# Rests of the tap matrices on one engine, and a gated channel tile split before it is put into token phases

## The chip, the core and the metric

One core of a Trainium2 chip runs the whole program. The metric is the device time of one execution in microseconds; the kernel before takes 1811.5 us (median of 3 runs, 1810.97 to 1811.91). TensorE does matrix products, VectorE, ScalarE and GpSimd elementwise work, SyncE issues the loads of the weights.

## The reference, cut to what matters

Two blocks of a model follow each other on 512 tokens of width 1024, all in fp32. The part that the change touches is the conformer convolution in the first block:

```python
def conformer_conv(h, w_pw1, b_pw1, w_dw, b_dw, ln_g, ln_b, w_pw2, b_pw2):
    u = h @ w_pw1 + b_pw1
    a, g = jnp.split(u, 2, axis=-1)
    u = a * jax.nn.sigmoid(g)
    u = depthwise_conv(u, w_dw) + b_dw        # 31 taps over the tokens, each channel by itself
    u = jax.nn.silu(layer_norm(u, ln_g, ln_b))
    return u @ w_pw2 + b_pw2
```

## The kernel before

Tensors lie with channels on the 128 partitions and the 512 tokens along the row, so 1024 channels are eight channel tiles. To get fp32 accuracy from the faster fp32r products, each factor is held as a head (rounded to fp32r by a ScalarE copy) and a rest (the value minus its head, a subtraction); a product is three matmuls, head by head, head by rest, rest by head (lines 358 to 360). `split` (line 392) makes such a pair of an activation: ScalarE writes the head (398), VectorE the rest (399).

Weights come in blocks of 512 columns, four 128-column pieces each. One load on SyncE (272) brings two blocks, 512 KB, into one of three `raw` buffers. For each block ScalarE copies the head into one of nine `W` buffers (285), and VectorE or GpSimd subtracts to give the rest (287); `on_pool` names the blocks whose rests GpSimd makes. A `raw` buffer is free when head and rest of both its blocks are made. The instructions of an engine are laid out ahead of time by a planner that works from the order of the program text, and run in that order.

The stage in question runs from about 649 to 772 us:

- TensorE multiplies by `pw1` (channel tiles 2 to 7, two gemms of 24 matmuls each, 512 columns). Behind each pair, `glu` multiplies both results by the row scales (1135, 1136), takes the sigmoid (451, called from 1137), and adds the bias and gates.
- Channel tiles 0 to 3 are convolved on VectorE: 31 instructions each (1078, 1083), handed out in small portions by `tick`. The first portions fall between the `pw1` gemms, the others between the tap matmuls.
- Channel tiles 4 to 7 are convolved on TensorE by `run_pe` after the last `pw1` gemm: tap matrices (`taps`, 128 pieces in 32 blocks, in 16 loads) multiply the gated tile. For that, even and odd tokens of 64 channels lie one above the other on the 128 partitions (two token phases, half as many columns: 256). Each tile takes 2 halves x 16 matrices x 3 = 96 matmuls of 256 columns; ScalarE then writes the sums back with the bias (1130, four instructions a tile).
- `conv_pe` prepares these tiles. Before the change VectorE gates straight into the phases (1111, four instructions on 64 partitions x 256), ScalarE takes the head of the whole (1113) and VectorE the rest (1114).
- The layer norm follows: TensorE adds up the columns of all eight tiles (1181) as soon as the last of them is written, ScalarE scales this to the mean (1192), and so on up to the `pw2` gemms.

Before the change GpSimd makes the rests of all `pw1` blocks from channel tile 2 on and of every second block of tap matrices; VectorE makes those of the other 16 blocks and of all later ones.

Of the kernel before, what the change touches and what calls it, by code (L numbers as in the profile page):

```python
# [11 lines left out]
F32 = mybir.dt.float32  # L12
F32R = mybir.dt.float32r
BF16 = mybir.dt.bfloat16
I32 = mybir.dt.int32
AF = mybir.ActivationFunctionType
OP = mybir.AluOpType
# [142 lines left out]
def pack(plan):  # L160

    blocks, cols = [[]], 0
    for piece in plan:
        if cols + piece[3] > 512:
            blocks.append([])
            cols = 0
        blocks[-1].append(piece)
        cols += piece[3]
    return [blocks[:1], blocks[1:2]] + [blocks[i:i + 2] for i in range(2, len(blocks), 2)]
# [75 lines left out]
class Weights:  # L245
# [4 lines left out]
    def __init__(self, prog, blob, raw_pool, w_pool):  # L250
        self.prog, self.nc, self.blob, self.raw_pool, self.w_pool = prog, prog.nc, blob, raw_pool, w_pool
        self.loads, self.blocks, self.loc, off = [], [], {}, 0
        for load in pack(make_plan()):
            start = 0
            for blk in load:
                c = 0
                for name, k, t, w in blk:
                    self.loc[name, k, t] = (len(self.blocks), c, w)
                    c += w
                self.blocks.append((len(self.loads), start, c))  # L260
                start += c
            self.loads.append((off, start))
            off += 128 * start
        self.raw, self.w, self.ndma, self.nsplit, self.cur = {}, {}, 0, 0, -1

        tiles = [self.loc["pw1", 7, 9][0] + 1, self.loc["taps", 0, 0][0], self.loc["pw2", 0, 0][0]]
        self.on_pool = set(range(tiles[0], tiles[1])) | set(range(tiles[1], tiles[2], 2))

    def dma(self):
        off, cols = self.loads[self.ndma]  # L270
# [34 lines left out]
class Program:  # L305
# [757 lines left out]
    def conformer(self, x, h, ps4, rs, first):  # L1063
        nc = self.nc
        V, A, G, mm, W = nc.vector, nc.scalar, nc.gpsimd, nc.tensor.matmul, self.W
        vv = self.pairs()
        late, mixed = [], []

        def conv_dve(c, up, dst, taps, bias):

            box = {}

            def tap(t):
                w, u = self.v("dw", 31 * c + t), up[:, t:t + T]
                if t == taps[0]:
                    acc = box["acc"] = self.PS()
                    if bias:
                        V.tensor_scalar(out=acc, in0=u, scalar1=w, scalar2=self.v("bdw", c), op0=OP.mult, op1=OP.add)
                    else:
                        V.tensor_scalar(out=acc, in0=u, scalar1=w, scalar2=None, op0=OP.mult)  # L1080
                else:
                    acc = box["acc"]
                    V.scalar_tensor_tensor(out=dst if dst is not None and t == taps[-1] else acc, in0=u, scalar=w,  # L1083
                                           in1=acc, op0=OP.mult, op1=OP.add)

            return [lambda t=t: tap(t) for t in taps], box

        def conv_pool(c, up, dst, taps):
            def tap(t):
                w, u = self.v("dw", 31 * c + t), up[:, t:t + T]  # L1090
                if t == taps[0]:
                    A.activation(out=dst, in_=u, func=AF.Identity, scale=w, bias=self.v("bdw", c))
                    return
                p = self.S()[:, :T]
                A.activation(out=p, in_=u, func=AF.Copy, scale=w)
                G.tensor_add(out=dst, in0=dst, in1=p)

            return [lambda t=t: tap(t) for t in taps]

        def conv_pe(c, a, g):  # L1100


            up = self.wide(F32)[:, :544].rearrange("p (h t) -> p h t", h=2)
            uh, ul = (self.wide(F32R)[:, :544].rearrange("p (h t) -> p h t", h=2) for _ in range(2))
            G.memset(up[:, :, 0:8], 0.0)
            G.memset(up[:, :, 263:272], 0.0)
            a, g = (x.rearrange("p (t f) -> p f t", f=2) for x in (a, g))
            for i in range(2):
                r = slice(64 * i, 64 * i + 64)
                for o, f, t in ((slice(0, 64), 1, 8), (slice(64, 128), 0, 7)):  # L1110
                    V.scalar_tensor_tensor(out=up[o, i, t:t + 256], in0=a[r, f], scalar=self.v("bp1", c)[r],
                                           in1=g[r, f], op0=OP.add, op1=OP.mult)
            A.activation(out=uh, in_=up, func=AF.Copy)
            V.tensor_sub(out=ul, in0=up, in1=uh.bitcast(F32))
            late.append((c, uh, ul))

        def run_pe():
            for i, (c, uh, ul) in enumerate(late):
                sums = self.PS().rearrange("p (h t) -> p h t", h=2)
                for g in range(2):  # L1120
                    for s in range(16):
                        self.mm3(sums[:, g], W("taps", s, 2 * i + g), (uh[:, g, s:s + 256], ul[:, g, s:s + 256]),
                                 s == 0, s == 15)
                        if s % 8 == 7:
                            self.tick(*TICK2)
                out = vv[c].rearrange("p (t f) -> p f t", f=2)
                for g in range(2):
                    for b in range(2):
                        r = slice(64 * b, 64 * b + 64)
                        A.activation(out=out[64 * g:64 * g + 64, b], in_=sums[r, g], func=AF.Identity,  # L1130
                                     bias=self.v("bd2", 2 * i + g)[r])

        def glu(c, za, zg):
            a, g = self.S()[:, :T], self.S()[:, :T]
            V.tensor_mul(out=g, in0=zg, in1=rs)  # L1135
            V.tensor_mul(out=a, in0=za, in1=rs)
            self.fn(SIGMOID, out=g, in_=g, func=AF.Sigmoid, bias=self.v("bp1", 8 + c))
            if CONV[c] == "E":
                return conv_pe(c, a, g)
            up = self.wide(F32)  # L1140
            G.memset(up[:, 0:15], 0.0)
            G.memset(up[:, 527:542], 0.0)
            V.scalar_tensor_tensor(out=up[:, 15:527], in0=a, scalar=self.v("bp1", c), in1=g,
                                   op0=OP.add, op1=OP.mult)
            if CONV[c] == "P":
                self.bg2.append(conv_pool(c, up, vv[c], range(31)))
            elif CONV[c] == "V":
                self.bg.append(conv_dve(c, up, vv[c], range(31), True)[0])
            else:
                self.bg2.append(conv_pool(c, up, vv[c], range(MIX)))  # L1150
                taps, part = conv_dve(c, up, None, range(MIX, 31), False)
                self.bg.append(taps)
                mixed.append((c, part))
# [3 lines left out]
        rs = rs()  # L1157
        self.tables(SIGMOID)
        glu(0, ps4[0], ps4[1])
        glu(1, ps4[2], ps4[3])  # L1160
        for c in range(2, 8):
            if c > 2:
                za = self.PS()
                self.gemm(za, "pw1", c, h)
                self.tick(*TICK)
            zg = self.PS()
            self.gemm(zg, "pw1", 8 + c, h)
            glu(c, za, zg)
            self.tick(*TICK)
        run_pe()  # L1170
        self.drain()
        for c, part in mixed:
# [570 lines left out]
```

## Time and profile before

| | |
|---|---|
| median of 3 runs | 1811.5 us |
| the profiled execution | 1812.31 us |
| its span, first to last instruction | 1810.6 us |
| TensorE busy | 1757.6 us, 97% |
| VectorE busy | 1113.1 us, 61% |
| ScalarE busy | 792.1 us, 44% |
| GpSimd busy | 250.6 us, 14% |

In the views PE is TensorE's matmul, PEld its weight load, DVE VectorE, ACT ScalarE, POOL GpSimd, SP SyncE (SPq its queue). `L287` is line 287. Busy shares are means over a program of many stages, so a stage is read with the views of its own stretch. Instructions of one engine overlap a little at their ends: what one costs in a row of the same kind is the distance from start to start, slightly less than its duration. The records of one execution give the durations; that execution took 0.8 us more than the median of the runs.

### The profile page before, as it was taken

Reading aid. Unit: us, or ns where it says so; the run is one execution under the profiler, and the core shown is the slowest. Engines: PE = TensorE matmul, PEld = TensorE weight load, DVE = VectorE, ACT = ScalarE, POOL = GpSimd, SP = SyncE. Lnnn points to the kernel's source line nnn. Section 1 sums busy time; section 2 is a strip of 40 time slices with the busy share of each in tenths; the row PEclk is TensorE's granted clock in tenths of the full one; section 3 lists DMA queues with packets and bytes.
Section 4 is the critical chain, followed back from the end, with each engine's and each line's share of the span. In section 5 each row is a group of like instructions: output and inputs, shape, how many; then the busy total and the mean of one; then the engine's idle time right before and its main releaser. Section 6 shows DMA issues by size and latency. Waiting matters only on the chain.

```text
span 1810.6 us, 23137 instructions
## 1 busy us (share of the span) xinstructions
PE 1757.6 (97%) x8828; PEld 1463.8 (81%) x8828; DVE 1113.1 (61%) x1798; ACT 792.1 (44%) x1445; POOL 250.6 (14%) x315
## 2 busy tenths in 40 slices
PE   9999999999999998999999999989999999999999
PEld 7778888888888976888888888888687888888887
DVE  7988685344444889967634444477997554344442
ACT  6546554333333532485533332346665433232330
POOL 3413330000000452303000000033223200000000
PEclk9999999999999999999999999999999999999999
DMA  6232223222222131421322222222222222222221
GB/s 202 64 99 65 94 71 105 93 96 99 97 93 94 47 117 43 156 94 59 118 93 95 98 99 94 93 75 89 83 60 93 95 94 97 99 94 94 93 93 59
DMA packets 49888, 167.26 MB, mean 92 GB/s; under 512 B 6848, under 2 KB 7296, under 8 KB 49776
## 3 DMA queue, kind: packets, MB, share of 16 engines
q1 hardware_dynamic: 47776, 160.70, 26.9%
q0 software_dynamic: 1936, 5.07, 1.0%
q8 instruction: 69, 1.13, 0.3%
q14 instruction: 43, 0.35, 0.1%
q10 hardware_dynamic: 64, 0.02, 0.0%
HBM read 158.25 MB, written 4.19 MB: 90 GB/s over the span
## 4 chain that ended last, share of the span: by engine, by line
PE 73%; DVE 18%; issue 4%; ACT 3%; POOL 2%; DMA 1%; SPq 0%; POOLq 0%; ACTq 0%; DVEq 0%
PE ps L359 24%; PE ps L358 24%; PE ps L360 23%; DVE ps L1083 4%; DVE W L287 2%; DVE P L969 1%; PE ps L624 1%; DVE P L402 1%; DVE P L399 1%; ACT S L451 1%; DMA raw<-in_w 1%; POOL P L972 1%; DVE S L1481 1%; DVE S L425 1%; DVE S L423 1%
## 5 line engine op out<-in xcount | busy, mean ns | idle before, releaser
L360 PE MATMUL ps<-P,W 128*128 128x512 f32 (+1 forms) x2541 | 935.2, 368 | 10.4 <-DVE W L287 10.1
L358 PE MATMUL ps<-P,W 128*128 128x512 f32 (+1 forms) x2541 | 938.2, 369 | 5.7 <-DVE S L1135 2.1
L359 PE MATMUL ps<-P,W 128*128 128x512 f32 (+1 forms) x2541 | 934.5, 368 | 5.9 <-DVE P L402 5.9
L285 ACT ACTIVATE W<-raw 128x512 fp32r<-128x512 f32 x578 | 357.7, 629 | 698.5 <-PE ps L360 588.9
L287 DVE TENSOR_TENSOR W<-raw,W 128x512 fp32r<-128x512 f32 x539 | 385.3, 722 | 397.8 <-ACT W L285 394.2
L360 PEld LDWEIGHTS ps<-P,W 128*128 128x128 f32 x2541 | 482.7, 190 | 96.8 <-DVE W L287 12.7
L358 PEld LDWEIGHTS ps<-P,W 128*128 128x128 f32 x2541 | 483.1, 190 | 91.9 <-DVE S L1135 2.5
L359 PEld LDWEIGHTS ps<-P,W 128*128 128x128 f32 x2541 | 482.9, 190 | 90.0 <-DVE P L402 6.8
L972 POOL TENSOR_TENSOR P<-P 128x256 f32<-128x256 f32 x48 | 45.4, 954 | 789.2 <-DVE P L969 788.1
L399 DVE TENSOR_TENSOR P<-S,P 128x512 fp32r<-128x512 f32 (+1 forms) x130 | 91.1, 707 | 50.5 <-ACT P L398 49.9
L398 ACT ACTIVATE P<-S 128x512 fp32r<-128x512 f32 (+1 forms) x130 | 78.9, 613 | 59.8 <-DVE S L1668 25.9
L1083 DVE SCALAR_TENSOR_TENSOR ps<-P,vec,ps 128x512 f32<-128x512 f32 x116 | 78.8, 746 | 0.1
L1030 DVE SCALAR_TENSOR_TENSOR S<-ps,S 128x512 f32<-128x512 f32 x64 | 43.7, 690 | 37.0 <-PE ps L360 36.7
L401 ACT ACTIVATE P<-P,vec 128x256 fp32r<-128x256 f32 (+1 forms) x80 | 43.7, 549 | 49.1 <-POOL P L972 29.5
L287 POOL TENSOR_TENSOR W<-raw,W 128x512 fp32r<-128x512 f32 x39 | 52.9, 1368 | 77.1 <-ACT W L285 74.0
L402 DVE SCALAR_TENSOR_TENSOR P<-P,vec 128x256 fp32r<-128x256 f32 (+1 forms) x80 | 53.2, 679 | 9.5 <-ACT P L401 9.4
L471 POOL TENSOR_TENSOR S<-S 128x256 f32<-128x256 f32 (+1 forms) x45 | 47.5, 1056 | 76.5 <-ACT S L470 74.1
L470 ACT ACTIVATE S<-P 128x256 f32<-128x256 f32 (+1 forms) x105 | 46.4, 473 | 17.9 <-DVE P L1057 11.8
L637 POOL TENSOR_TENSOR P<-S,P 128x512 fp32r<-128x512 f32 (+1 forms) x24 | 34.2, 1426 | 112.6 <-DVE P L636 95.7
L1050 DVE TENSOR_TENSOR P<-ps,P 128x512 f32<-128x512 f32 x42 | 29.1, 692 | 30.9 <-PE ps L360 30.9
L624 PE MATMUL ps<-P 128*128 128x512 f32 (+3 forms) x160 | 41.3, 376 | 1.2 <-DVE S L1447 0.8
L471 DVE TENSOR_TENSOR S<-S 128x256 f32<-128x256 f32 (+1 forms) x60 | 33.1, 551 | 14.2 <-ACT S L470 13.2
(263 smaller groups left out, 1303.2 us busy)
## 6 DMA issues: line engine op xcount, KB each, us to landing
raw<-in_w SPq DMA_DIRECT2D x286, 512.0 KB
P<-in_xT SPq DMA_DIRECT2D x8, 256.0 KB
P<-in_xT POOLq DMA_DIRECT2D x8, 256.0 KB, 5.1
keep<-P SPq DMA_DIRECT2D x8, 256.0 KB
P<-P SPq DMA_DIRECT2D x16, 128.0 KB
P<-keep POOLq DMA_DIRECT2D x8, 256.0 KB, 5.2
out<-P SPq DMA_DIRECT2D x7, 256.0 KB
raw<-in_w SPq DMA_DIRECT2D x2, 256.0 KB
```

The costliest lines, as they stand in the source:

```text
L285: nc.scalar.activation(out=w[:, 0, :cols], in_=r, func=AF.Copy)
L287: eng.tensor_sub(out=w[:, 1, :cols], in0=r, in1=w[:, 0, :cols].bitcast(F32))
L358: mm(ps, w[0], x[0], start=first, stop=False)
L359: mm(ps, w[0], x[1], start=False, stop=False)
L360: mm(ps, w[1], x[0], start=False, stop=last)
L398: nc.scalar.activation(out=hi, in_=src, func=AF.Copy)
L399: nc.vector.tensor_sub(out=lo, in0=src, in1=hi.bitcast(F32))
L402: nc.vector.scalar_tensor_tensor(out=lo, in0=src, scalar=scale, in1=hi.bitcast(F32), op0=OP.mult, op1=OP.subtract)
L471: (eng or nc.vector).tensor_add(out=acc, in0=acc, in1=t)
L624: mm(o[:m], k, q[:, pl, c0:], start=n == 0 and m == 128, stop=n == len(keys) - 1 and mask is None)
L972: ins = eng.tensor_add(out=x[k][:, cols], in0=x[k][:, cols], in1=m[k][:, cols]).ins
L1083: V.scalar_tensor_tensor(out=dst if dst is not None and t == taps[-1] else acc, in0=u, scalar=w, in1=acc, op0=OP.mult, op1=OP.add)
```

## The change

The rests of all 32 blocks of tap matrices go to GpSimd (those of the `pw1` blocks were there before). In `glu`, a channel tile for TensorE is gated in one VectorE instruction on 128 partitions x 512, in token order, and split as a whole by `split` (one ScalarE copy, one VectorE subtraction). Four ScalarE copies then move head and rest together into the phases, each of 64 partitions x 2 x 256, into two tiles `x[0]` and `x[1]`, whose margins GpSimd sets to zero (four small memsets instead of two). `run_pe` reads the same values from the new tiles.

```diff
@@ class Weights
-        tiles = [self.loc["pw1", 7, 9][0] + 1, self.loc["taps", 0, 0][0], self.loc["pw2", 0, 0][0]]
-        self.on_pool = set(range(tiles[0], tiles[1])) | set(range(tiles[1], tiles[2], 2))
+        self.on_pool = range(self.loc["pw1", 7, 9][0] + 1, self.loc["pw2", 0, 0][0])
@@ conformer
-        def conv_pe(c, a, g):
-            up = self.wide(F32)[:, :544].rearrange("p (h t) -> p h t", h=2)
-            uh, ul = (self.wide(F32R)[:, :544].rearrange("p (h t) -> p h t", h=2) for _ in range(2))
-            G.memset(up[:, :, 0:8], 0.0)
-            G.memset(up[:, :, 263:272], 0.0)
-            a, g = (x.rearrange("p (t f) -> p f t", f=2) for x in (a, g))
+        def conv_pe(c, u):
+            n = self.split(self.P(), u).rearrange("p l (t f) -> p f l t", f=2)
+            x = [self.wide(F32R)[:, :544].rearrange("p (l t) -> p l t", l=2) for _ in range(2)]
             for i in range(2):
                 r = slice(64 * i, 64 * i + 64)
+                G.memset(x[i][:, :, 0:8].bitcast(F32), 0.0)
+                G.memset(x[i][:, :, 263:272].bitcast(F32), 0.0)
                 for o, f, t in ((slice(0, 64), 1, 8), (slice(64, 128), 0, 7)):
-                    V.scalar_tensor_tensor(out=up[o, i, t:t + 256], in0=a[r, f], scalar=self.v("bp1", c)[r],
-                                           in1=g[r, f], op0=OP.add, op1=OP.mult)
-            A.activation(out=uh, in_=up, func=AF.Copy)
-            V.tensor_sub(out=ul, in0=up, in1=uh.bitcast(F32))
-            late.append((c, uh, ul))
+                    A.activation(out=x[i][o, :, t:t + 256], in_=n[r, f], func=AF.Copy)
+            late.append((c, x))
@@ run_pe
-            for i, (c, uh, ul) in enumerate(late):
+            for i, (c, x) in enumerate(late):
...
-                        self.mm3(sums[:, g], W("taps", s, 2 * i + g), (uh[:, g, s:s + 256], ul[:, g, s:s + 256]),
+                        self.mm3(sums[:, g], W("taps", s, 2 * i + g), (x[g][:, 0, s:s + 256], x[g][:, 1, s:s + 256]),
@@ glu
             if CONV[c] == "E":
-                return conv_pe(c, a, g)
+                V.scalar_tensor_tensor(out=a, in0=a, scalar=self.v("bp1", c), in1=g, op0=OP.add, op1=OP.mult)
+                return conv_pe(c, a)
```

## Rows read from the trace of the kernel before

**Rows 1.** The page's first part: busy time, share, instructions of each engine.

```profile
PE 1757.6 (97%) x8828; PEld 1463.8 (81%) x8828; DVE 1113.1 (61%) x1798; ACT 792.1 (44%) x1445; POOL 250.6 (14%) x315
```

**Rows 2.** Stretches: length, busy of PE, PEld, DVE, ACT, POOL, granted clock, DMA share, GB/s.

```profile
649.00:706.60 57.60, 57.41 (x240) 46.45 (x241) 57.28 (x87) 16.70 (x27) 21.57 (x22) 0.97 0.20 65
706.60:767.80 61.20, 50.77 (x389) 48.53 (x387) 61.09 (x93) 25.85 (x45) 17.24 (x13) 0.94 0.42 137
```

**Rows 3.** Timeline of PE, 706 to 774: start, duration, instruction, idle before and releaser.

```profile
706.60 0.28 PE L358 MATMUL ps<-P,W 128*128 128x256 f32 x1
...
710.05 0.29 PE L359 MATMUL ps<-P,W 128*128 128x256 f32 x1
713.34 0.38 PE L360 MATMUL ps<-P,W 128*128 128x256 f32 x1 [2.99 <-DVE W L287]
...
716.18 0.28 PE L359 MATMUL ps<-P,W 128*128 128x256 f32 x1
722.01 0.58 PE L360 MATMUL ps<-P,W 128*128 128x256 f32 x1 [5.55 <-DVE W L287]
...
767.56 0.28 PE L360 MATMUL ps<-P,W 128*128 128x256 f32 x1
770.41 3.08 PE L1181 MATMUL ps<-P,onesf 128*128 128x256 f32 x12 [2.57 <-DVE P L1083]
```

**Rows 4.** A stretch of PE alone: length, busy, granted clock, DMA share, GB/s.

```profile
722.00:725.00 3.00, 2.99 (x14) 0.50 0.52 175
```

**Rows 5.** Timeline of DVE, the same columns as the timeline of PE.

```profile
711.67 1.61 DVE L287 TENSOR_TENSOR W<-raw,W 128x512 fp32r<-128x512 f32 x1
713.21 0.68 DVE L1135 TENSOR_TENSOR S<-ps,S 128x512 f32<-128x512 f32 x1
...
721.28 0.68 DVE L287 TENSOR_TENSOR W<-raw,W 128x512 fp32r<-128x512 f32 x1
721.88 2.72 DVE L1083 SCALAR_TENSOR_TENSOR ps<-P,vec,ps 128x512 f32<-128x512 f32 x4
...
769.62 1.39 DVE L1083 SCALAR_TENSOR_TENSOR P<-P,vec,ps 128x512 f32<-128x512 f32 x2
```

**Rows 6.** Groups of DVE by line, 648.4 to 771.1: count, busy, mean ns, idle before.

```profile
L287 DVE TENSOR_TENSOR W<-raw,W 128x512 fp32r<-128x512 f32 x20 | 15.6, 786 | 0.0
L1111 DVE SCALAR_TENSOR_TENSOR P<-S,vec 64x256 f32<-64x256 f32 x16 | 9.5, 597 | 0.2
...
L1114 DVE TENSOR_TENSOR P<-P 128x544 fp32r<-128x544 f32 x4 | 3.9, 976 | 0.1
L1143 DVE SCALAR_TENSOR_TENSOR P<-S,vec 128x512 f32<-128x512 f32 x4 | 3.8, 951 | 0.0
```

**Rows 7.** Timeline of POOL.

```profile
711.47 1.26 POOL L287 TENSOR_TENSOR W<-raw,W 128x512 fp32r<-128x512 f32 x1 [12.90 <-ACT W L285]
...
726.13 1.29 POOL L287 TENSOR_TENSOR W<-raw,W 128x512 fp32r<-128x512 f32 x1 [7.33 <-ACT W L285]
...
754.57 1.76 POOL L287 TENSOR_TENSOR W<-raw,W 128x512 fp32r<-128x512 f32 x1 [3.63 <-ACT W L285]
```

**Rows 8.** Timeline of ACT.

```profile
725.42 1.15 ACT L285 ACTIVATE W<-raw 128x512 fp32r<-128x512 f32 x2 [6.96 <-DMA raw<-in_w]
...
767.88 1.48 ACT L1130 ACTIVATE P<-ps,vec 64x256 f32<-64x256 f32 x3 [1.34 <-PE ps L360]
...
770.04 0.49 ACT L1130 ACTIVATE P<-ps,vec 64x256 f32<-64x256 f32 x1
...
773.64 0.38 ACT L1192 ACTIVATE S<-ps 128x256 f32<-128x256 f32 x1
```

**Rows 9.** Waits of SP's queue, 690 to 771: total, times, longest.

```profile
SPq L272 <- DVE W L287: 77.0, 17, 21.6
```

**Rows 10.** Timeline of SP: the load that lands at 725.4.

```profile
722.10 0.33 SPq L272 DMA_DIRECT2D raw<-in_w  x1
```

**Rows 11.** DMA in 40 slices of 735 to 768: GB/s of each.

```profile
GB/s 15 154 382 99 0 55 313 268 0 30 283 323 0 20 243 367 5 45 204 343 35 74 263 328 0 70 273 293 10 0 194 397 45 5 204 412 15 30 268 338
```

## Prediction, made before the changed kernel was run

> **What bounds the kernel now.** The first part of the page [rows 1] says that TensorE is busy for 97% of the span, so a change can only win where TensorE waits. The table by stretches [rows 2] shows where: in the `pw1` stretch (649 to 706.6) PE has no gap to speak of, but in that of the tap matrices PE is busy 50.8 of 61.2 us, while DVE is busy 57.3 of 57.6 and 61.1 of 61.2 us in the two. VectorE has not been idle since 649: it is behind, and stays behind.
>
> The timeline of PE [rows 3] gives the size. From 706.60 to 710.05 there are 30 tap matmuls, so one costs 3.45 / 29 = 0.119 us. There are 4 tiles x 2 halves x 16 matrices x 3 = 384; undisturbed they end at 706.6 + 45.7 = 752.3. The last one starts at 767.56, so the run ends at 767.7, 15.4 us late. Gaps of 3.29 and 5.83 us between starts (8.9 us beyond the cadence), both released by a rest of VectorE's (L287), make up most of it. Behind the longer one the clock stands at half speed, 14 matmuls in 3.00 us [rows 4], which costs 14 x (0.214 - 0.119) = 1.3 us. The other 5 us are small waits: VectorE puts four taps (2.72) and one rest in each turn, 721.28 to 724.5 or 3.24 us [rows 5], and one turn releases two blocks, which PE uses in 24 x 0.119 = 2.86 us. Then PE waits for VectorE's last tap: column means start at 770.41, and the last tap of channel tile 3 is written at 769.62 + 1.39 = 771.0 [rows 3, 5].
>
> The same engine holds the loads. SyncE waited 77.0 us for VectorE's rests, once for 21.6 [rows 9]: a `raw` buffer is free only when both rests are made. A load issued at 722.10 is copied by ScalarE from 725.42 [rows 8, 10], so it lands in 3.3 us, and ScalarE then idles until the next one is allowed to go.
>
> **The change, part by part.**
>
> *Rests.* VectorE loses 16 of them. In a row with taps one costs 0.60 us (721.28 to 721.88) [rows 5]; the mean of its 20 in this stage is 0.786 [rows 6], because some wait. I take 0.70, or 11 us in all. GpSimd gains 16 at 1.26 to 1.29 us, once 1.76 [rows 7]. It then makes each block alone: 1.29 against PE's 12 x 0.119 = 1.43. That is close, but it does not start level: nine `W` buffers let heads and rests run up to eight blocks ahead of PE, and during `pw1` a block lasts twice as long on PE. So 24 blocks remain at 706.6: 24 x 1.29 = 31 us at best, 24 x 1.76 = 42 at worst, both under 45.7. GpSimd's queue holds nothing else here but small memsets. I take no stall; the high end is rival A.
>
> *Loads.* With rests made at once, a buffer's turn is 3.3 (landing) + 0.6 (first head) + 2 x 1.29 + about 0.15 (issue) = 6.6 us; three buffers give a load each 2.2 us, and PE wants one each 2.86. That needs 524 KB / 2.86 us = 183 GB/s. The slices of the stage reach 382 and 412 GB/s and stand near zero in between [rows 11], so the room is there.
>
> *Gating and splitting.* For four tiles VectorE now spends 9.5 + 3.9 = 13.4 us (L1111, L1114) [rows 6]. Afterwards each tile costs a gate as in L1143, 0.7 us undisturbed and 0.95 on its mean with waits, and a rest of 0.6: 1.3 a tile, 5.2 in all, 8.2 less. Bounds: 5.0 and 7.0.
>
> *Copies into phases.* Sixteen on ScalarE that the trace does not show. The nearest rows: 128 x 512 from SBUF 0.58 each (two in 1.15), 64 x 256 from PSUM 0.49 [rows 8]; so 0.6 to 1.0 for 64 x 512, I take 0.65. A tile adds 2.6 us to ScalarE, 10.4 in all; its load in the tap stretch was 25.9 of 61.2 us [rows 2], which hides it. They wait for VectorE's rest of the tile, and heads of weight blocks queue behind them; what covers that is the blocks already made. Tile 7, the last, is wanted by PE only at 706.6 + 288 x 0.119 = 740.9. Cost 0; without the cover, up to 3 us in tile 7's turn. The two more memsets a tile run on GpSimd while it waits for heads.
>
> *Where VectorE then stands.* Before, it reached tile 7's products at 713.21 [rows 5], 6.6 us behind PE. Ahead of that point it loses three tiles' savings (3 x 2.05) and two rests (0.6, and 1.54 for that at 711.67): 8.3 us. It would be there at 704.9, so it now waits for PE's 706.6. From 713.2 to 771.0 it worked 57.8 us; without tile 7's 2.05 and 14 rests at 0.70 that is 46.0: last tap at 752.6. If the planner fills the short idle time with taps, 751; if tile 7's gate and rest both wait for GpSimd, 755.
>
> *Where TensorE then stands.* Taps 706.6 to 752.3 without stall or slow clock. ScalarE's first write-back followed the last matmul's start by 0.32 us; four of 0.5 and one head in between end at 755.2 (754.6 without the head) [rows 8]. So what is late next is no longer VectorE but TensorE with its write-back: all eight tiles are there at 755.2 instead of 771.0, 15.8 us earlier. Before, five of the eight column sums followed that moment, now one: 4 x 0.21 = 0.8 more (12 in 3.08 less a wait of 0.6) [rows 3]. Sum: 16.6 us. What comes behind (mean, squares, `pw2`) is untouched and moves forward as one piece. ScalarE's mean at 773.64 [rows 8] came 1.5 us behind its sum, since two heads stood ahead of it; whether that stays is unknown, 0 to 1.5 us of further gain.
>
> The profiled execution took 1812.3: 1812.3 - 16.6 = 1795.7. Its time is 0.8 above the median of the runs, so 1795 for the median.
>
> *A rule that speaks against it.* The VectorE rest at 711.67 began 0.2 us behind GpSimd's of 711.47 and took 1.61 us instead of 0.68, ending 0.55 us after GpSimd's [rows 5, 7]. VectorE's taps, with one operand in PSUM, do not show this, and GpSimd's rest at 726.13 ran its 1.29 among them. The Trainium skill, SBUF — State Buffer, section Who interferes with whom, has the rule: a VectorE instruction with two SBUF inputs and a GpSimd instruction that reads SBUF exclude each other for a whole instruction. The trace agrees. By it each gate and each rest of a tile may wait up to 1.3 us for the busier GpSimd, which is the 755 above; the sum stands, since 755.2 ends later.
>
> **Rivals.**
>
> A. *The supply of rests paces the taps.* For it: each block now depends on one engine of 1.29 us behind a ScalarE whose queue has got longer. Against: the head start. If only five blocks are ready at 706.6 and head and rest follow each other without overlap (0.6 + 1.29 = 1.9), 27 x 1.9 = 51.3, plus the last block and the write-back 4.3: 762.2, a gain of 9.6, 1802.
>
> B. *VectorE still ends last.* First rests of `pw2` blocks stay on it and stand among the last taps. If it waits a landing (3.3) there twice, 752.6 + 6.6 = 759.2, a gain of 11.8: about 1800. For it: the planner orders by estimates. Against: VectorE's 61.1 of 61.2 us leave no such wait in the trace [rows 2].
>
> C. *The time comes back.* The column sums start earlier but `pw2`'s blocks do not, and PE idles there: gain under 3.6, 1808 to 1812. Against: their loads hang on the `raw` buffers, which come free earlier.
>
> D. *Slower: one load at a time.* The place is the ring of `raw` buffers. In the trace of this stage loads never overlap: one each 3.24 us, landing in 3.3. If they could not overlap, the 13 of 16 tap loads left at 706.6 would take 13 x 6.6 = 86 us: taps end near 793, some 25 us later than before, 1836. It decides from (767.7 - 706.6) / 13 = 4.7 us a load on. Against: it was VectorE that spaced them, and bursts of 400 GB/s are there.
>
> **How the numbers follow.** Forecast 0.62 (its own range 1791.5 to 1797.5: the stretch from 706.6 to 770.4 less 45.7 leaves 18.1 us, plus 1.5 at the mean, at best; 14 at least), A 0.17, B 0.07, C 0.06, D 0.08. From 1791.5 to 1806 lie the forecast, A and B, some 0.83. A measurement of this kernel tells 0.2%, 3.6 us, from no change: faster 0.86, same 0.06 (C), slower 0.08 (D).
>
> **What would show it.** Right: no PE gap on L287 between 706 and 752, no half clock there, loads closer than 3 us, VectorE idle just ahead of 706.6, GpSimd at 1.3 us a block, and column sums near 755 released by ScalarE's L1130. Wrong: PE waiting for POOL L287 (A), the sums released by L1083 after 757 (B), a longer wait of PE for `pw2` blocks behind the column sums than before (C), ScalarE waiting over 4 us for each load (D).

## The result, and the profile after

| | kernel before | kernel after |
|---|---|---|
| time, median (lowest to highest) | 1811.24 us (1809.79 to 1811.91) | 1791.35 us (1788.58 to 1794.69) |
| ratio after / before, 95% interval | | 0.9892 (0.9874 to 0.9910) |
| profiled execution, its span | 1812.31, 1810.6 us | 1788.58, 1786.8 us |

The kernel became 1.1% faster. The forecast was 1795, with a range from 1791.5 to 1806; the median stands 0.15 us below that range, 3.65 us below the forecast. Measured a second time (the experiment `after_again` below) the same kernel took 1794.61. So most of the question is why the stage gained what it did, and a small part is where the rest of the first measurement's 20 us comes from.

The first part of the page of after (busy time, share of the span, instructions; compare [rows 1]):

```profile
PE 1746.1 (98%) x8828; PEld 1455.2 (81%) x8828; DVE 1092.6 (61%) x1770; ACT 802.0 (45%) x1461; POOL 272.4 (15%) x339
```

VectorE lost 28 instructions, ScalarE and GpSimd gained 16 and 24. A stretch of after (length, busy of PE, PEld, DVE, ACT, POOL, granted clock, DMA share, GB/s; compare [rows 2]):

```profile
703.50:751.50 48.00, 48.00 (x396) 47.74 (x395) 46.94 (x72) 30.09 (x53) 32.16 (x29) 1.00 0.51 162
```

From the first tap matmul to the end of the last write-back TensorE is busy for all of 48.0 us at full clock, where it was busy 50.8 of 61.2 us at a granted clock of 0.94 [rows 2]. GpSimd works 32 us of the 48 where it worked 17 of 61. The timeline of PE of after (start, duration, instruction, idle before and releaser, as in all timelines here; compare [rows 3]):

```profile
703.47 0.28 PE L357 MATMUL ps<-P,W 128*128 128x256 f32 x1
...
749.16 0.28 PE L359 MATMUL ps<-P,W 128*128 128x256 f32 x1
749.28 3.62 PE L1177 MATMUL ps<-P,onesf 128*128 128x256 f32 x16
```

The first and the last tap start 45.7 us apart, just 383 times the cadence of 0.119, and the column sums follow without a gap. In before the same two stand 61.0 us apart, and TensorE then idled for 2.57 us until the sums [rows 3]. The timeline of DVE of after (compare [rows 5]):

```profile
706.02 0.68 DVE L1130 TENSOR_TENSOR S<-ps,S 128x512 f32<-128x512 f32 x1
...
711.22 31.69 DVE L1082 SCALAR_TENSOR_TENSOR ps<-P,vec,ps 128x512 f32<-128x512 f32 x48
...
747.26 1.40 DVE L1082 SCALAR_TENSOR_TENSOR P<-P,vec,ps 128x512 f32<-128x512 f32 x2
```

The product of tile 7 (L1130; L1135 in before) comes 2.6 us behind the first tap matmul instead of 6.6, the 48 taps that follow stand in one row with no rest among them, and VectorE's last tap ends at 748.66, ahead of TensorE. ScalarE of after, from the phase copies of tile 7 (L1109) to the mean copy (L1188; compare [rows 8]):

```profile
710.86 2.73 ACT L1109 ACTIVATE P<-P 64x512 fp32r<-64x512 f32 x4
...
749.48 2.00 ACT L1125 ACTIVATE P<-ps,vec 64x256 f32<-64x256 f32 x4 [3.90 <-PE ps L359]
751.81 1.15 ACT L284 ACTIVATE W<-raw 128x512 fp32r<-128x512 f32 x2 [0.33 <-DMA raw<-in_w]
752.98 0.38 ACT L1188 ACTIVATE S<-ps 128x256 f32<-128x256 f32 x1
```

The copies cost 2.73 / 4 = 0.68 each. The write-back starts 0.32 us behind the last tap's start and is done at 751.48, 48.0 us after the first tap. It does not end the stage: TensorE's 16 matmuls of column sums, two to a tile, run from 749.28 to 752.90 without a gap, the two of the last tile start at 752.30, and the write-back is done 0.8 us before that. The mean copy follows the sums at 752.98; the two heads that still stand ahead of it end at the same moment. GpSimd of after (compare [rows 7]), then the loads in SyncE's queue (compare [rows 10]), then what that queue waited for from 690 to 760 (total, times, longest; compare [rows 9]):

```profile
714.39 13.81 POOL L286 TENSOR_TENSOR W<-raw,W 128x512 fp32r<-128x512 f32 x11 [1.25 <-ACT W L284]
```

```profile
720.74 0.33 SPq L271 DMA_DIRECT2D raw<-in_w  x1
723.23 0.33 SPq L271 DMA_DIRECT2D raw<-in_w  x1
```

```profile
SPq L271 <- POOL W L286: 44.1, 14, 6.9
```

Eleven rests in 13.81 us are 1.26 each, and GpSimd waits for heads, not the other way round. Where loads follow each other they now go out each 2.5 us; the 15 from 705.0 to 749.3 are 3.2 us apart on the mean, where 16 in before, from 707.3 to 765.3, are 3.9. What they wait for is GpSimd's rest where it was VectorE's for 77.0 us.

**Where the time came from.** From the first tap matmul to the mean copy, before takes 773.64 - 706.60 = 67.0 us [rows 3, 8], after 752.98 - 703.47 = 49.5: 17.5 us. A mark that every kernel has is a pair of ScalarE's table loads ahead of and behind the stage, the sigmoid's and the layer norm's. "Stage" below is the time between their starts. Timeline of ACT in before and, in the second fence, in after:

```profile
646.02 1.28 ACT L442 ACT_TABLE_LOAD   x1
...
779.95 1.28 ACT L442 ACT_TABLE_LOAD   x1
```

```profile
642.71 1.28 ACT L441 ACT_TABLE_LOAD   x1
...
759.29 1.28 ACT L441 ACT_TABLE_LOAD   x1
```

133.9 against 116.6 us, 17.3 less. The spans differ by 23.8, so 6.5 us come from elsewhere, although outside this stage each engine's instructions are the same in the same order. One candidate is the granted clock. A window of before around 1385, where another stage ends (columns as in the table by stretches), then the one of after around the same work:

```profile
1375.00:1395.00 20.00, 16.96 (x88) 13.74 (x88) 13.94 (x19) 13.42 (x24) 12.14 (x14) 0.83 0.32 99
```

```profile
1352.00:1372.00 20.00, 16.67 (x92) 13.50 (x92) 14.72 (x20) 13.89 (x25) 12.14 (x14) 0.91 0.30 97
```

Summed over windows of 5 us, TensorE stood at half clock for 37 us of the execution of before, 27 of them outside the stage, and for 14 us of that of after, none in the stage. 14 us of half clock less outside are worth up to 7 us of work. Whether that is where the 6.5 us come from, and whether the change has a part in it, is what `after_again` and `before_again` test.

### The profile page after: what moved, and what is told of

It is laid out like the page before. It is cut to its first block, busy times and chain, and to the rows that moved or that the text cites. A ratio compares the mean times of both kernels' runs of the same rounds, so it can differ in the third digit from the quotient of the medians.

```text
span 1786.8 us, 23140 instructions
## 1 busy us (share of the span) xinstructions
PE 1746.1 (98%) x8828; PEld 1455.2 (81%) x8828; DVE 1092.6 (61%) x1770; ACT 802.0 (45%) x1461; POOL 272.4 (15%) x339
## 4 chain that ended last, share of the span: by engine, by line
PE 81%; DVE 11%; issue 3%; ACT 2%; POOL 2%; DMA 1%; SPq 0%; POOLq 0%; DVEq 0%; ACTq 0%
PE ps L358 26%; PE ps L357 26%; PE ps L359 26%; DVE P L968 2%; DVE W L286 1%; PE ps L623 1%; DVE P L401 1%; DVE S L424 1%; POOL P L971 1%; ACT S L450 1%; DVE S L1477 1%; DVE P L398 1%; DVE S L422 1%; DMA P<-in_xT 1%; DVE P L636 0%
## 5 line engine op out<-in xcount | busy, mean ns | idle before, releaser
L286 DVE TENSOR_TENSOR W<-raw,W 128x512 fp32r<-128x512 f32 x523 | 372.2, 719 | 396.8 <-ACT W L284 391.1
L398 DVE TENSOR_TENSOR P<-S,P 128x512 fp32r<-128x512 f32 (+3 forms) x134 | 93.8, 705 | 50.5 <-ACT P L397 49.9
L397 ACT ACTIVATE P<-S 128x512 fp32r<-128x512 f32 (+3 forms) x134 | 81.4, 613 | 63.2 <-DVE S L1664 25.8
L286 POOL TENSOR_TENSOR W<-raw,W 128x512 fp32r<-128x512 f32 x55 | 73.6, 1369 | 38.0 <-ACT W L284 33.9
```

The costliest lines, as they stand in the source:

```text
L286: eng.tensor_sub(out=w[:, 1, :cols], in0=r, in1=w[:, 0, :cols].bitcast(F32))
L397: nc.scalar.activation(out=hi, in_=src, func=AF.Copy)
L398: nc.vector.tensor_sub(out=lo, in0=src, in1=hi.bitcast(F32))
```

## The experiments

Ratios are against the kernel before on the same chip (median 1811.03 beside rests_only, gate_only, after_again and before_again, 1812.44 beside the other four), with 95% intervals; the stage is that of the profiled execution.

| kernel | time, us | ratio | stage, us |
|---|---|---|---|
| before, first profile | 1811.24 | | 133.9 |
| after, first profile | 1791.35 | 0.9892 (0.9874 to 0.9910) | 116.6 |
| rests_only | 1803.22 | 0.9950 (0.9937 to 0.9962) | 128.3 |
| gate_only | 1801.27 | 0.9943 (0.9930 to 0.9957) | 125.6 |
| copies_twice | 1795.80 | 0.9906 (0.9881 to 0.9930) | 118.8 |
| rests_slow | 1805.97 | 0.9959 (0.9946 to 0.9972) | 128.6 |
| rests_psum_gate | 1801.29 | 0.9934 (0.9914 to 0.9955) | 123.1 |
| v2 | 1793.78 | 0.9895 (0.9875 to 0.9914) | 115.3 |
| after_again | 1794.61 | 0.9907 (0.9891 to 0.9922) | 115.8 |
| before_again | 1811.57 | 1.0003 (0.9993 to 1.0013) | 135.0 |

**rests_only: the rests on GpSimd, the gates and tiles as before.**

```diff
-        tiles = [self.loc["pw1", 7, 9][0] + 1, self.loc["taps", 0, 0][0], self.loc["pw2", 0, 0][0]]
-        self.on_pool = set(range(tiles[0], tiles[1])) | set(range(tiles[1], tiles[2], 2))
+        self.on_pool = range(self.loc["pw1", 7, 9][0] + 1, self.loc["pw2", 0, 0][0])
```

> The rests of all tap matrices on GpSimd, gating and splitting as in the kernel before. Theory of the prediction (VectorE is behind from 649 us on, and its last tap ends the stage): TensorE no longer waits for rests, its tap matmuls end 45.7 us behind their start, but VectorE loses only the 16 rests, 11.2 us, so its last tap comes at about 759.8 on the clock of the profile before and the column sums wait for it, some 5 us behind TensorE. From the sigmoid's table load to the layer norm's the stage took 133.9 us before and 116.6 after; here 122.7. Time 1800 (ratio 0.994). Rival (only the waits of TensorE for rests cost time; what is left on VectorE is hidden): all of the gain is here, stage 116 to 118, time 1791 to 1794 (ratio 0.989 to 0.990).

Measured: 128.3, a gain of 5.6 us. Both forecasts missed, the rival's by more. TensorE still waits for VectorE, once for a rest and then with its column sums for the last tap (timelines of PE and of DVE of this kernel):

```profile
756.22 0.39 PE L359 MATMUL ps<-P,W 128*128 128x256 f32 x1 [3.78 <-DVE W L286]
...
760.72 4.42 PE L1180 MATMUL ps<-P,onesf 128*128 128x256 f32 x12 [2.45 <-DVE P L1082]
...
759.93 1.39 DVE L1082 SCALAR_TENSOR_TENSOR P<-P,vec,ps 128x512 f32<-128x512 f32 x2
```

The rest is that of a block with the last three tap matrices and the first one of `pw2`, which `on_pool` leaves to VectorE. It is VectorE's in after too, so not quite all rests of tap matrices moved; there it is made in time (742.82).

From the start of the stage VectorE's last tap ends 118.4 us later, against 125.0 in before: 6.5 us earlier, though 16 rests at 0.70 (11 us) are gone. Groups of DVE by line (count, busy, mean ns, idle before; compare [rows 6]) show where the gain went:

```profile
L1110 DVE SCALAR_TENSOR_TENSOR P<-S,vec 64x256 f32<-64x256 f32 x16 | 10.5, 656 | 0.2
...
L1113 DVE TENSOR_TENSOR P<-P 128x544 fp32r<-128x544 f32 x4 | 6.8, 1712 | 0.1
```

The four rests of tiles cost 1712 ns each where they cost 976, the 16 gates 656 where they cost 597: 2.9 + 0.9 = 3.8 us. With 1.65 for a pair shown next that is 5.5, where 4.5 are missing: the 16 rests had cost VectorE nearer 0.75 us each than 0.70. A tile's rest in the timeline and two instructions of the stage's start, with GpSimd's rows of the same moments:

```profile
643.61 1.55 DVE L422 SCALAR_TENSOR_TENSOR S<-S 128x512 f32<-128x512 f32 x1
645.19 1.64 DVE L424 SCALAR_TENSOR_TENSOR S<-S 128x512 f32<-128x512 f32 x1
...
694.82 1.82 DVE L1113 TENSOR_TENSOR P<-P 128x544 fp32r<-128x544 f32 x1
...
639.57 5.04 POOL L286 TENSOR_TENSOR W<-raw,W 128x512 fp32r<-128x512 f32 x4
644.87 3.09 POOL L286 TENSOR_TENSOR W<-raw,W 128x512 fp32r<-128x512 f32 x2 [0.26 <-ACT W L284]
694.76 4.29 POOL L286 TENSOR_TENSOR W<-raw,W 128x512 fp32r<-128x512 f32 x3 [2.60 <-ACT W L284]
```

The tile's rest starts 0.06 us behind a rest of GpSimd's that takes 1.3, and ends 1.88 behind that start, 0.6 after it. L422 and L424 read two SBUF operands too; here they meet GpSimd and take 3.2 us together, in before 0.85 + 0.69. That pair depends on chance and not on the kernel: it took 1.33 + 1.71 in before_again, 1.40 + 1.64 in after, twice 0.69 in after_again, gate_only, rests_psum_gate and v2. Where VectorE is behind, it moves the end of the stage by up to 1.7 us between executions; without it rests_only would gain some 7. So GpSimd's added work is paid for in part by VectorE's instructions with two SBUF operands. The mechanism stood in the prediction (the rest at 711.67 [rows 5, 7]); its price for the old gates and tile rests did not.

**gate_only: the new gates, splits and copies, the rests as before.**

```diff
-        self.on_pool = range(self.loc["pw1", 7, 9][0] + 1, self.loc["pw2", 0, 0][0])
+        tiles = [self.loc["pw1", 7, 9][0] + 1, self.loc["taps", 0, 0][0], self.loc["pw2", 0, 0][0]]
+        self.on_pool = set(range(tiles[0], tiles[1])) | set(range(tiles[1], tiles[2], 2))
```

(against after.)

> Gating whole, splitting whole and ScalarE's copies into phases as in the changed kernel, the rests dealt out as before (every second one of the tap matrices on VectorE). Theory of the prediction: VectorE loses 8.2 us, TensorE still goes in step with VectorE's turns of four taps and one rest, the gaps on L287 stay but the first two shrink; the stage takes 133.9 - 8.2 = 125.7 us, time 1803 (ratio 0.9955). Rival (only TensorE's waits for rests cost time): no gain beyond 2 us, ratio 0.999 to 1.000.

Measured: 125.6, as the theory forecast. VectorE is 8 us less behind, but still behind. Waits of PE from 700 to 771 (total, times, longest):

```profile
PE ps L360 <- DVE W L287: 3.5, 4, 2.1
PE ps L1178 <- DVE P L1083: 2.6, 1, 2.6
```

TensorE waits for VectorE's rests, and then its sums wait for VectorE's last tap. So neither part alone brings VectorE ahead of TensorE; together they do. The parts gain 5.6 (some 7 without the collision by chance) and 8.3 us of stage, 14 to 15.5 in sum, and together 17.3. VectorE's last tap, counted from the start of the stage, ends at 125.0 us in before, 118.4 in rests_only, 116.9 here and 105.9 in after: 6.5 and 8.1 us earlier alone, 19.0 together. The times of all runs do not show that the whole is more than its parts: by the medians 7.8 + 9.8 = 17.6 us against 16.4 for after_again, beside the same runs of before. So it is a reading of VectorE's rows in single executions, and not shown as a gain in time. A cause for what is over in those rows shows in after's groups of DVE:

```profile
L1134 DVE SCALAR_TENSOR_TENSOR S<-S,vec 128x512 f32<-128x512 f32 x4 | 3.3, 814 | 0.0
L398 DVE TENSOR_TENSOR P<-S,P 128x512 fp32r<-128x512 f32 x4 | 2.7, 681 | 0.0
```

Eight instructions of 0.75 on the mean stand there instead of 20 that met a busier GpSimd at 656 and 1712 ns: the new gates and splits save 17.3 - 6.0 = 11.3 us against rests_only, where against before they save 13.4 - 6.0 = 7.4.

**rests_psum_gate: as rests_only, with one operand of each gate left in PSUM.**

```diff
-            a, g = self.S()[:, :T], self.S()[:, :T]
+            a, g = za, self.S()[:, :T]
```

(against rests_only.)

> The kernel with only the rests moved (rests_only), and the product of the first half with the row scales left in PSUM, so that VectorE's gates read one operand from SBUF instead of two. In rests_only VectorE gained 6.5 us between the sigmoid's table load and its last tap instead of the 11.2 that the moved rests are worth: the rests of the tiles took 1.71 us each instead of 0.98 and the gates 0.66 instead of 0.60. Theory (a VectorE instruction with two SBUF operands and a GpSimd rest hold each other up for the whole instruction, and GpSimd now makes more of them): the gates fall back to 0.48 to 0.50 us each, all sixteen alike, VectorE gains some 2.5 us on them; the tiles' rests, still with two SBUF operands, stay at 1.3 to 1.8. The stage goes from 128.3 to about 125.8 us. Rival (these instructions are long for another reason, the 64-partition pattern or VectorE's own order): the gates keep a mean of 0.60 or more with single ones of 1.4.

Measured, groups of DVE by line:

```profile
L1110 DVE SCALAR_TENSOR_TENSOR P<-ps,vec,S 64x256 f32<-64x256 f32 x16 | 7.7, 481 | 0.2
...
L1113 DVE TENSOR_TENSOR P<-P 128x544 fp32r<-128x544 f32 x4 | 6.5, 1629 | 0.1
```

The same line by source, least/median/most ns of one, in rests_only and here:

```profile
L1110 DVE SCALAR_TENSOR_TENSOR P<-S,vec x16: 468/484/1422, 678.0 to 717.2; 64x256 f32<-64x256 f32 x16
```

```profile
L1110 DVE SCALAR_TENSOR_TENSOR P<-ps,vec,S x16: 466/483/491, 678.8 to 714.6; 64x256 f32<-64x256 f32 x16
```

With two SBUF operands the median gate costs 484 ns but the worst 1422; with one the worst costs 491. The tile rests, whose operands are still both in SBUF, stay at 1629. That is the exclusion, shown by taking away one of its two conditions. The Trainium skill, SBUF — State Buffer, section Who interferes with whom, states that a VectorE instruction with two SBUF inputs contends with a GpSimd instruction that reads SBUF, and one with at most one does not. This case's runs agree. The stage fell by 5.2 us to 123.1 (forecast 125.8). The rows add up to 5.5, near that: 2.8 us at the gates, 0.3 at the tile rests, 0.6 at the gates of VectorE's own four tiles (L1142, 741 ns where they took 883), which the edit changes too, and 1.8 at the pair L422 and L424, which happened to meet no rest here (0.69 each). Without that luck the gain is some 3.4, where 2.5 was forecast.

**copies_twice: each phase copy on ScalarE made twice.**

```diff
-                    A.activation(out=x[i][o, :, t:t + 256], in_=n[r, f], func=AF.Copy)
+                    for _ in range(2):
+                        A.activation(out=x[i][o, :, t:t + 256], in_=n[r, f], func=AF.Copy)
```

> The changed kernel with each of ScalarE's sixteen copies into phases made twice (the second writes the same values again): 10.8 us more work on ScalarE. Theory of the prediction (these copies are hidden: ScalarE has slack and the blocks made ahead cover their place in its queue): stage 116.2 us within 0.8, time within 1 us of the changed kernel's. Rival (ScalarE's queue is close to setting the pace, since heads of weight blocks stand behind the copies): each tile's 2.7 us shows, in TensorE gaps on heads or GpSimd's rests, and the stage grows by 3 to 10 us.

Measured: 118.8, 2.2 to 2.9 us over the two profiles of after, for 16 x 0.68 = 10.9 us more of ScalarE. "Free" was off: the forecast was 116.2 within 0.8, the rival 3 to 10 us more, and the truth lies between. The copies of the last tile, and the end of the stage, with a row of PE last:

```profile
716.98 5.54 ACT L1110 ACTIVATE P<-P 64x512 fp32r<-64x512 f32 x8 [0.78 <-DVE P L398]
...
756.45 1.15 ACT L284 ACTIVATE W<-raw 128x512 fp32r<-128x512 f32 x2 [1.48 <-DMA raw<-in_w]
757.63 0.38 ACT L1189 ACTIVATE S<-ps 128x256 f32<-128x256 f32 x1
...
754.30 3.08 PE L1178 MATMUL ps<-P,onesf 128*128 128x256 f32 x12 [0.49 <-DVE P L1082]
```

The mean copy stands 51.6 us behind the first tap instead of 49.5. The taps took 46.6 instead of 45.7, with one gap of 0.8 on a rest. Then the column sums waited for VectorE's last taps, which ended 48.8 us behind the first tap matmul (45.2 in after), and ended at 757.38; the heads that had waited 1.48 for a load ended 0.2 later. VectorE is late here in part because its gate and rest of tile 7 met GpSimd, 1.56 and 1.72 us where after has 0.74 and 0.69. So at least three quarters of the doubled copies are hidden, and how much of the rest is ScalarE's is not separated. The single ones of the change leave no gap in TensorE's taps, so their cost there is none that these traces show.

**rests_slow: every second tap rest made twice on GpSimd.**

```diff
+        self.twice = range(self.loc["taps", 0, 0][0] + 1, self.loc["pw2", 0, 0][0], 2)
-            eng.tensor_sub(out=w[:, 1, :cols], in0=r, in1=w[:, 0, :cols].bitcast(F32))
+            for _ in range(2 if self.nsplit in self.twice else 1):
+                eng.tensor_sub(out=w[:, 1, :cols], in0=r, in1=w[:, 0, :cols].bitcast(F32))
```

> The changed kernel with every second rest of the tap matrices made twice by GpSimd (the same values again), so that a tap block costs it 1.9 us on the mean instead of 1.27, against TensorE's 1.43. Theory (GpSimd starts the tap blocks some eight ahead of TensorE, so only the blocks left at that time count): 25 blocks left at 704 and 12.5 of them twice make 37.5 x 1.27 = 47.6 us, the last rest comes near 752 instead of 740 on the clock of the profile after, TensorE waits some 4 us in all and the stage grows by 3 to 6 us, all of it near the end of the tap matmuls. Rival (no head start, GpSimd's pace is the stage's pace from the first tap block): 32 x 1.91 = 61 us against 45.7, the stage grows by 12 to 15.

Measured: 128.6, or 12.0 us more. The rival had the size, the theory forecast a quarter to a half of it. Neither had the loads that end the stage. GpSimd's timeline, and then the waits of all engines from 700 to 775:

```profile
716.29 41.34 POOL L288 TENSOR_TENSOR W<-raw,W 128x512 fp32r<-128x512 f32 x32
```

```profile
ACT W L285 <- DMA raw<-in_w: 24.2, 11, 4.5
...
PE ps L361 <- POOL W L288: 5.6, 6, 1.8
...
ACT P L1111 <- POOL P L1109: 4.3, 2, 2.3
```

At 1.5 x 1.29 = 1.9 us a block GpSimd never stops, and TensorE waits for it 6 times; its taps take 52.8 us instead of 45.7. I had taken the head start for enough: 24 blocks by 1.76 is 42. The traces show two things that this left out. ScalarE's copies wait for memsets that stand behind GpSimd's rests in order, and the loads wait for `raw` buffers that those rests hold. The second ends the stage:

```profile
762.37 1.15 ACT L285 ACTIVATE W<-raw 128x512 fp32r<-128x512 f32 x2 [4.48 <-DMA raw<-in_w]
763.54 1.97 ACT L1127 ACTIVATE P<-ps,vec 64x256 f32<-64x256 f32 x4
...
766.71 0.38 ACT L1190 ACTIVATE S<-ps 128x256 f32<-128x256 f32 x1
```

Heads for `pw2` stand ahead of the write-back in ScalarE's queue, and wait 4.48 us for their load. From the last tap's start (759.94) to the write-back's it takes 3.6 us instead of 0.32. So 7.1 of the 12 us come from slower taps, about 3 from the queue ahead of the write-back, and 2 from behind the mean copy, where the layer norm's wait for TensorE is 3.7 us long instead of 1.6. There the granted clock is the difference: from the mean copy to the table load (columns as in the table by stretches), first this kernel, where TensorE had been busy for 4.3 of the 6.8 us ahead, then after:

```profile
766.70:775.10 8.40, 6.77 (x22) 5.63 (x23) 4.08 (x11) 3.94 (x11) 0.00 (x0) 0.64 0.21 76
```

```profile
752.98:759.29 6.31, 4.68 (x22) 4.14 (x23) 4.07 (x11) 3.97 (x12) 0.00 (x0) 1.00 0.41 147
```

**v2: an attempt at something faster.** Two of the last tile's four write-backs on VectorE, and GpSimd's rests carried on to the first eight blocks of `pw2`.

```diff
-        self.on_pool = range(self.loc["pw1", 7, 9][0] + 1, self.loc["pw2", 0, 0][0])
+        self.on_pool = range(self.loc["pw1", 7, 9][0] + 1, self.loc["pw2", 7, 3][0] + 1)
...
+                        if i == len(late) - 1 and b:
+                            V.tensor_scalar(out=out[64 * g:64 * g + 64, b], in0=sums[r, g],
+                                            scalar1=self.v("bd2", 2 * i + g)[r], scalar2=None, op0=OP.add)
+                            continue
```

> The changed kernel, further on: two of the four write-backs of the last channel tile on VectorE instead of ScalarE, and GpSimd also makes the rests of the first eight pw2 blocks (9 with the one shared with the last taps). Theory (what ends the stage now is TensorE, then ScalarE's four write-backs of 0.5 us, then two heads of weight blocks that stand ahead of the mean): two write-backs run beside the other two, 1.0 us less, and raw buffers come free sooner, so that the heads are made before the last matmul and not ahead of the mean, 1.2 to 1.5 us less; the stage goes from 116.2 to about 114 us, time 2.2 us below the changed kernel's. Rival (VectorE's order or its rests of pw2 blocks set the end): no change, 116.

Measured: 115.3 in the stage and 0.9895, not told apart from after (116.6 and 115.8; 0.9892 and 0.9907). The write-backs of the two engines, ACT and then DVE, and the column sums of PE:

```profile
752.74 0.49 ACT L1129 ACTIVATE P<-ps,vec 64x256 f32<-64x256 f32 x1
753.78 0.49 ACT L1129 ACTIVATE P<-ps,vec 64x256 f32<-64x256 f32 x1 [0.56 <-DVE P L1126]
755.96 0.39 ACT L1192 ACTIVATE S<-ps 128x256 f32<-128x256 f32 x1 [1.68 <-PE ps L1181]
...
753.26 0.49 DVE L1126 TENSOR_SCALAR P<-ps,vec 64x256 f32<-64x256 f32 x1 [4.30 <-ACT P L1129]
...
752.30 3.62 PE L1181 MATMUL ps<-P,onesf 128*128 128x256 f32 x16
```

With a second row of DVE's at 754.31 they take turns instead of running side by side: all four write into one tile, and each waits for the one before. The heads ahead of the mean copy are gone, and it now waits 1.68 us for TensorE's sums. But neither could have gained anything to speak of. The sums follow the last tap in one row of 3.62 us here as in after, and the mean copy stands 49.5 us behind the first tap in both: what the edit shortens was covered by the sums before.

**after_again and before_again: the two kernels once more, unchanged.**

> The changed kernel once more, for a second profile and more times. Theory: of the 23.8 us between the two profiled spans 17.4 lie in the stage and return here (stage 116.6 us within 0.5), while the other 6.4 lie in stretches whose order of instructions is the same in both kernels and go with TensorE's clock, which stood at half speed for about 37 us in the profile before and 13 in the one after; here the half-speed time is another, and outside the stage the span moves with half of it. Rival: the change itself moves other stages, and these 6.4 us return here in the same places.

> The kernel before once more, for a second profile. Theory: stage 133.9 us within 1, half-speed time of TensorE outside the stage somewhere between 10 and 30 us and not at the same places as in the first profile. Rival: half-speed time and places as in the first profile of before (27 us outside the stage).

Measured: the stage comes back, 115.8 and 135.0, or 19.2 us apart where the first pair is 17.3; the mean copy comes 49.5 and 66.6 us behind the first tap, as before. Both stages lie just outside what was forecast (within 0.5 and 1); 1.5 us of before_again's are the pair L423 and L425 of its start. So the stage's 17 to 19 us belong to the change.

The first pair's other 6.5 us do not come back. The time outside the stage (span less stage) is 1676.7 and 1672.7 us in the two executions of before, 1670.2 and 1673.3 in the two of after, so the spans are 18.6 apart instead of 23.8. Half clock does not account for them as the theory has it. Outside the stage it is 27 and 17 us in before and 14 and 14 in after, and yet the two of after differ by 3.1 us. Over all ten traces the time outside lies between 1670.2 and 1677.1, and does not go with the half clock there: 1677.1 with 17 us of it (v2), 1674 and 1676 with 10 (copies_twice, rests_slow), 1673 with 27 (rests_only). Between ScalarE's table loads at 37 and at 210 us neither of the first two traces has any half clock, and before takes 173.1 us there, after 171.6. The expectation that the half clock of before_again falls in other places did not hold either: four of its five places outside the stage (near 612, 847, 1207 and 1387, each within 5 us) are those of the first profile. So the 6.5 us are a difference between single executions, and their cause is not shown.

## Why the prediction was right

*VectorE is behind, and holds TensorE and the loads: right.* Each part alone shifted VectorE and left TensorE waiting for it; both together brought it ahead, and the taps ran without a gap.

*VectorE loses 11 us of rests and 8.2 of gating: right in sum, for a reason that I had split wrongly.* Alone, the rests bring VectorE's last tap only 6.5 us forward, since GpSimd's share comes back as collisions with the old gates and tile rests. The new gates and splits are 8 instructions instead of 20, and one of them cost 0.81 and 0.68 (forecast 0.7, or 0.95 with waits, and 0.6), so they take most of the collisions away too. The gates' price alone came out as forecast, 8.1 us of VectorE's last tap in gate_only, and the rests' alone did not. Both together came near the forecast 19.2 (VectorE's last tap is 19.0 earlier), because the collisions that the rests bring are mostly with instructions that the other edit takes away.

*VectorE waits for TensorE from tile 7 on: right in its end, not in its way there.* The sign of it, VectorE idle just ahead of the first tap, did not come: VectorE reached tile 7 at 2.6 us behind the first tap and was busy up to it. The order of its instructions had changed: 66 of its 124 convolution instructions stand ahead of tile 7's products where 60 did, some 4.0 us, which the prediction had allowed for (its 751). Another 1.5 us went to the pair L422 and L424. Its last tap ended 45.2 us behind the first tap (forecast 46.0, or 44.4 with the taps filled in) and so ahead of the write-back.

*TensorE's taps 45.7, then the write-back: the taps right, what stands behind them wrong, and the sum right by luck in part.* It took 45.7 to the last tap's start, 48.0 to the end of the write-back (forecast 48.6, with a head among the four that was not there). In before the end of VectorE's last tap stood at 64.4: 16.4 us against the 15.8 of the forecast. But the write-back does not end the stage. The prediction had one column sum left behind it; in after all eight follow the last tap in one row of 3.6 us and cover the write-back, and the sign that ScalarE's L1130 releases the sums did not come. It also took a sum for 0.21 us, where each is two matmuls of 0.22: the 12 in 3.08 us of [rows 3] are six sums. A write-back that was counted and is hidden, and sums that were not counted, nearly cancel: to the mean copy it is 17.5 against 16.6 plus 0 to 1.5.

*Copies on ScalarE at 0 us: right.* 0.68 each (forecast 0.65), and some three quarters of as much again are hidden too.

*GpSimd makes each block in time: right, but the margin was mis-sized.* At 1.27 against TensorE's 1.43 there was no stall. I had argued that even 1.76 a block would do. At 1.9 the stage loses 12.0 us, because a late rest also holds a memset for ScalarE, a `raw` buffer, and through it the heads ahead of the write-back. The head start does not cover those.

*The forecast of 1795 against 1791.35.* The stage gave 17.3 where 16.6 was forecast, and 19.2 in the second pair. Most of what is missing to 3.65 us is not in the stage: the prediction carried the rest of one execution of before over to after, and outside the stage two executions of one kernel differ by 3 to 4 us. The second measurement, 1794.61, is 0.4 us from the forecast; so near a hit is luck beside such differences. The low end of the range was a little too low by its own terms: 1811.5 less 18.1 and 1.5 is 1791.9.

*The rivals.* A, paced by the supply, was not so at GpSimd's actual rate, and is what rests_slow made true. B: VectorE's last tap ends 0.8 us before the write-back starts, so it is not last, but is near. C: the layer norm's table load comes 20.7 us earlier (779.95 to 759.29), and so does the one at 805 in before, behind the first blocks of `pw2`: nothing came back. D: loads go out each 2.5 us in a row, less than the 3.3 that one took to land [rows 8, 10], and the stretch moves 162 GB/s where it moved 137 [rows 2]; they overlap. On the mean they are 3.2 us apart, so the sign "closer than 3 us" came only in part, and no TensorE gap followed from it.

What stays open is where the time outside the stage comes and goes, 1670 to 1677 us, and why the half clock at the ends of other stages differs from one execution to the next. The change may have a small part in it: the mean granted clock is 0.990 in 36 runs of before and 0.994 in 9 of after, some 14 us of half clock, of which 7 to 10 lie in the stage in the traces. No experiment here separates that.

## What to carry to other kernels

When an engine is behind for a whole stage, find how far behind it is and what stands next in line; a change pays up to that next limit. Look at the next limit as closely: here it was TensorE's column sums, and v2 worked on the write-back that they cover. Two edits can also touch each other: the one here took away collisions that the other had made. Before moving work to GpSimd, count the VectorE instructions with two SBUF operands that will run beside it: here moving 11 us of rests brought 6.5, and putting one operand in PSUM, or making fewer and wider instructions, got most of the rest back. An engine that works in order close to its consumer's rate has less margin than its mean says, since all else in its queue and all buffers that it holds are late with it.

## What the runs showed of the hardware that was not expected

- A VectorE instruction with two SBUF operands beside a busy GpSimd: 128x544 rests 976 ns with half of the blocks' rests on GpSimd, 1712 with all of them; 64x256 gates up to 1422 ns, and at most 491 with one operand in PSUM.
- The time that TensorE stands at half clock was 37 and 27 us in two executions of before (27 and 17 of it outside the stage), 14 and 17 in two of after (14 and 14). Outside the stage the order of instructions is the same in all four, and the time there differs by up to 6.5 us and does not go with it.
- One 64x512 copy on ScalarE from SBUF costs 0.68 us, more than the 0.58 of a 128x512 head [rows 8]. The copy reads every second value of a row and the head all of them; which of the differences costs is not separated.
- Two VectorE instructions at the stage's start (L422, L424; L423, L425 in before) took 1.4 to 1.6 us together in some executions and 3.0 to 3.2 in others, by whether a rest of GpSimd's ran beside them.
